# The first stage of a float32 transformer block: products on rows that are not scaled yet, and rows scaled ahead of the transposition

## The chip, the cores and the metric

One core of a Trainium2 chip runs the kernel. The metric is the device time of one execution, in microseconds (us); lower is better. Of the kernel before there are three timed runs, with a median of 1368.38 us (1367.94 to 1368.66), and one profiled execution.

## The reference

```python
h = rmsnorm(x, norm_w)              # x: (512, 2048) float32
proj = h @ w_in                     # w_in: (2048, IN_WIDTH), cut into eleven parts:
(a_q, a_f, a_i, a_g, c_q, c_kv, k_idx_raw, w_idx_raw, b_g, m_a, m_b) = split(proj)
y_a = hgrn2_branch(a_q, a_f, a_i, a_g, ...)   # gated linear recurrence, 8 heads
y_b = dsa_branch(c_q, c_kv, k_idx_raw, w_idx_raw, b_g, ...)   # indexed sparse attention
merged = sigmoid(m_a) * (y_a @ w_pa) + sigmoid(m_b) * (y_b @ w_pb)
return rmsnorm(x + merged @ w_out, final_norm_w)

def rmsnorm(x, w):
    return x * rsqrt(mean(x * x, axis=-1) + EPS) * w
```

All is float32. The first stage of the kernel computes `h`, transposed, and the first 272 columns it needs of `proj`: 256 of `a_i` (head pair 0) and the 16 of `w_idx_raw`.

## The kernel before, in words

**Numbers.** A float32 operand `a` is held as two parts that TensorE takes at one pass each: a high part (`high`, `w_high`: a rounding copy on ScalarE) and a low part, `a` minus the high part (`low`, `w_low`). A product is then three: high x high (here "hh"), low x high ("lh") and high x low ("hl"). In the stage, `xh` and `xl` hold the two parts of the normalised input, transposed, with 2048 channels in 16 blocks of 128 on the partitions; four blocks make a group `g`, 0 to 3. `wh` and `wl` hold those of the weights, again four blocks for each `i`.

**The first stage** is the function `start` (from L250 on). The 512 rows of `x` are four tiles `t` of 128 rows. Each tile is loaded in two halves (`xs[t][i]`, 512 KB each). A tile goes through these steps:

- `square`, `rstd` (L298 to L303): the sum of squares of its two halves on ScalarE, then a sum on VectorE and a root on ScalarE; `on_diag` takes the reciprocal and puts it on the diagonal of a 128x128 matrix.
- `turn` (L309 to L315): 16 transpositions on TensorE into four PSUM banks, one for each group.
- `spread` (L337 to L342): a product of a matrix of ones with the diagonal, so that the 128 row factors lie along the free dimension (`rrow`).
- the scaling on VectorE: each transposed element times its channel's weight `wc` (a column of `norm_w`) times its row's factor; the first tile does it in two steps (`weigh`, and `scaled` at L398), the others in one (L350, one instruction for each block, 16 for a tile).
- `high` on ScalarE and `low` (L324), for the tiles after the first on GpSimd for odd groups and on VectorE for even ones.
- `project` (L371 to L385): for each group, hh, lh and hl of four products each, 48 for a tile, into one PSUM bank; then the sums are moved out: 256 columns by ScalarE to `v` (L384) and 16 by VectorE to `widx` (L385).

`project(t)` writes the next tile's `follow(t + 1)` (its transpositions, spread, scaling, squares) between its second and its third group, so TensorE's queue holds 24 products of tile `t`, 16 transpositions and a spread of tile `t + 1`, and the other 24 products. In the last tile `prep(0)` stands there, which splits the weights of the next job.

**Order.** The program is compiled with a schedule by hand: every engine runs its instructions in the order in which the code writes them, and waits in that order where an operand is not ready. Semaphores come from the tiles' reads and writes.

**Loads.** All stand in SyncE's queue in this order: `norm_w`, tile 0 of `x`, weights 0 and 1, tile 1, weights 2 and 3, tiles 2 and 3, six small ones into `rows`, and the weights of the next job.

**Space.** TensorE's transpositions use a PSUM pool of four banks (`bank`), which also holds `warm`, a tile that four products of ones write ahead of the first load (L290 to L292). The sums use another four.

After the stage, `rows` is transposed (L432), and the jobs follow, which all read `xh` and `xl`.

Of the kernel before, what the change touches and what calls it, by code (L numbers as in the profile page):

```python
# [26 lines left out]
F32 = mybir.dt.float32  # L27
FR = mybir.dt.float32r
AF = mybir.ActivationFunctionType
OP = mybir.AluOpType  # L30
# [4 lines left out]
T, D = 512, 2048  # L35
# [15 lines left out]
def hybrid_block(ctx, tc, x, norm_w, w_in, lb_table, gnorm_a, q_norm_w, kv_norm_w, w_uq,  # L51
# [3 lines left out]
    V, A, G, PE, SP = nc.vector, nc.scalar, nc.gpsimd, nc.tensor, nc.sync  # L55
# [7 lines left out]
    mmp = ctx.enter_context(tc.tile_pool(name="mmp", bufs=4, space=PSUM))  # L63
# [4 lines left out]
    def bank(name):  # L68
        return sdp.tile([128, 512], F32, name=name, tag="sd")
# [10 lines left out]
    def mm(ps, l, r, first, last):  # L80
        PE.matmul(ps, l, r, start=first, stop=last, skip_group_check=True)  # L81
# [168 lines left out]
    def start():  # L250
        R.v0 = enter("v0")
        p0 = enter("p0", side="right")
        ident = p0.tile([128, 128], F32, name="ident")
        A.dma_start(ident, c_ident)
        HF = D // 2
        nw = p0.tile([16, 128], F32, name="nw")
        wc = p0.tile([128, 16], F32, name="wc")
        xs = [[p0.tile([128, HF], F32, name=f"x{t}{i}") for i in range(2)] for t in range(4)]
        ys = [p0.tile([128, 4, 128], F32, name=f"y{g}") for g in range(4)]
        diag = p0.tile([128, 128], F32, name="diag")  # L260
        sq = p0.tile([128, HF], mybir.dt.bfloat16, name="sq")
        st = p0.tile([128, 4, 4], F32, name="st")
        rows = p0.tile([128, 128], F32, name="rows")
        G.memset(rows, 1.0)
        G.tensor_copy(ones_r, rows)
        wh = [p0.tile([128, 4, 272], FR, name=f"fh{i}") for i in range(4)]
        wl = [p0.tile([128, 4, 272], FR, name=f"fl{i}") for i in range(4)]
        raw = [None] * 4

        def load_x(t):  # L270
            for i in range(2):
                SP.dma_start(xs[t][i], x2[t * 128:(t + 1) * 128, i * HF:(i + 1) * HF])

        def load_w(i):
            raw[i] = p0.tile([128, 4, 272], F32, name=f"fr{i}")
            for o, c0, c1 in ((0, 2048, 2304), (256, 4992, 5008)):
                SP.dma_start(raw[i][:, :, o:o + c1 - c0],
                             w_in[i * 512:(i + 1) * 512, c0:c1].rearrange("(k p) n -> p k n", p=128))

        SP.dma_start(nw, norm_w.rearrange("o (k d) -> (o k) d", d=128))  # L280
        load_x(0)
        load_w(0)
        load_w(1)
        load_x(1)
        load_w(2)
        load_w(3)
        load_x(2)
        load_x(3)
        A.activation(st[:, 0, 0:1], eps, AF.Sqrt)
        warm = bank("warm")  # L290
        for _ in range(4):
            PE.matmul(warm[:, 0:128], ones, ones, start=True, stop=True)  # L292
        G.memset(rows, 0.0)
        pw = mmp.tile([128, T], F32, name="acc")
        PE.transpose(pw[:, 0:16], nw, ident[0:16, 0:16])
        V.tensor_copy(wc, pw[:, 0:16])

        def square(t, i):  # L298
            A.activation(sq, xs[t][i], AF.Square, accum_out=st[:, t, i:i + 1])

        def rstd(t):
            V.tensor_add(st[:, t, 2:3], st[:, t, 0:1], st[:, t, 1:2])
            A.activation(st[:, t, 2:3], st[:, t, 2:3], AF.Sqrt, bias=eps, scale=1.0 / D)  # L303

        def on_diag(t):
            V.reciprocal(st[:, t, 3:4], st[:, t, 2:3])
            V.tensor_scalar(diag, ident, st[:, t, 3:4], None, op0=OP.mult)

        def turn(t, g):  # L309
            pt = bank("pt")  # L310
            for j in range(4):
                k = g * 4 + j
                PE.transpose(pt[:, j * 128:(j + 1) * 128],  # L313
                             xs[t][k // 8][:, (k % 8) * 128:(k % 8) * 128 + 128], ident)
            return pt  # L315

        def weigh(pt, g):
            V.tensor_tensor(ys[g], pt.rearrange("p (j t) -> p j t", j=4),
                            wc[:, g * 4:g * 4 + 4, None].to_broadcast([128, 4, 128]), op=OP.mult)

        def high(t, g):
            A.activation(xh[g][:, :, t * 128:t * 128 + 128], ys[g], AF.Copy)

        def low(t, g):  # L324
            o = slice(t * 128, t * 128 + 128)
            (G if t and g % 2 else V).tensor_tensor(xl[g][:, :, o], ys[g], xh[g][:, :, o].bitcast(F32),
                                                    op=OP.subtract)

        def w_high(i):
            A.activation(wh[i], raw[i], AF.Copy)  # L330

        def w_low(i, eng):
            eng.tensor_tensor(wl[i], raw[i], wh[i].bitcast(F32), op=OP.subtract)

        v = hg[0, "v"] = R.v0.tile([128, 4, 256], F32, name="hv")

        def spread():  # L337
            pr = mmp.tile([128, T], F32, name="acc")
            PE.matmul(pr[:, 0:128], ones, diag, start=True, stop=True)
            r = p0.tile([128, 128], F32, name="rrow", bufs=2)  # L340
            V.tensor_copy(r, pr[:, 0:128])
            return r  # L342

        def follow(t):
            pts = [turn(t, g) for g in range(4)]
            r = spread()

            def scaled(g):
                for j in range(4):
                    V.scalar_tensor_tensor(ys[g][:, j, :], pts[g][:, j * 128:j * 128 + 128],  # L350
                                           wc[:, g * 4 + j:g * 4 + j + 1], r, op0=OP.mult, op1=OP.mult)
                high(t, g)

            scaled(0)
            scaled(1)
            low(t, 0)
            if t < 3:
                square(t + 1, 0)
            scaled(2)
            low(t, 1)  # L360
            if t < 3:
                square(t + 1, 1)
            scaled(3)
            if t < 3:
                rstd(t + 1)
            low(t, 2)
            if t < 3:
                on_diag(t + 1)
            low(t, 3)

        def project(t):  # L371
            o = slice(t * 128, t * 128 + 128)
            acc = mmp.tile([128, T], F32, name="acc")
            for g in range(4):
                if g == 2:
                    if t < 3:
                        follow(t + 1)
                    else:
                        prep(0)
                for n, (xp, wp) in enumerate(((xh, wh), (xl, wh), (xh, wl))):  # L380
                    for k in range(4):
                        mm(acc[:, 0:272], xp[g][:, k, o], wp[g][:, k, :], g + n + k == 0,
                           g + n + k == 8)
            A.activation(v[:, t, :], acc[:, 0:256], AF.Copy)  # L384
            V.tensor_copy(widx[:, t, :], acc[:, 256:272])  # L385

        pts = [turn(0, g) for g in range(4)]
        weigh(pts[0], 0)
        weigh(pts[1], 1)
        square(0, 0)  # L390
        square(0, 1)
        rstd(0)
        on_diag(0)
        w_high(0)
        weigh(pts[2], 2)
        r = spread()

        def scaled(g):  # L398
            V.tensor_tensor(ys[g], ys[g], r[:, None, :].to_broadcast([128, 4, 128]), op=OP.mult)
            high(0, g)  # L400

        scaled(0)
        scaled(1)
        w_low(0, V)
        w_high(1)
        low(0, 0)
        weigh(pts[3], 3)
        square(1, 0)
        scaled(2)
        low(0, 1)  # L410
        scaled(3)
        w_low(1, V)
        w_high(2)
        w_low(2, V)
        square(1, 1)
        low(0, 2)
        rstd(1)
        low(0, 3)
        on_diag(1)
        w_high(3)  # L420
        w_low(3, G)
        SP.dma_start(rows[0:16], lb_table.rearrange("a (h d) -> (a h) d", d=128))
        SP.dma_start(rows[16:20], q_norm_w.rearrange("o (k d) -> (o k) d", d=128))
        SP.dma_start(rows[20:22], kv_norm_w.rearrange("o (k d) -> (o k) d", d=128))
        SP.dma_start(rows[22:23], kidx_norm_w)
        SP.dma_start(rows[23:24], kidx_norm_b)
        SP.dma_start(rows[24:25], gnorm_a)
        load_ahead()
        for t in range(4):
            project(t)  # L430
        pt = bank("pt")
        PE.transpose(pt[:, :128], rows, ident)  # L432
        V.tensor_copy(cols[:, 0:25], pt[:, :25])
        leave("p0")
# [1128 lines left out]
```

## Time and profile before

| | |
|---|---|
| median of three timed runs | 1368.38 us |
| profiled execution | 1367.72 us |
| its span, first to last instruction | 1365.8 us |
| TensorE, matmul busy | 1347.4 us |
| VectorE busy | 1075.2 us |
| ScalarE busy | 656.7 us |
| GpSimd busy | 81.2 us |
| transposition of `rows`, behind the first stage | starts at 46.67 us |

How to read the profile. It tells of one execution. Times count from the first instruction. PE is TensorE's matmul, PEld its weight loads, DVE is VectorE, ACT ScalarE, POOL GpSimd, SP the queue that issues the loads. A row of the timeline gives the start, the length, the engine, the line of the code (L313), the operation, what it writes and reads, how many neighbours of the kind are taken together (x16) and, in brackets, how long the engine sat idle before and what ended that. A group's row has the count, the busy time in us, the mean of one in ns, and the idle time before. The rows by stretches give, for each engine, busy us and instructions, then the granted clock of TensorE (1.00 is full), the share of DMA time and GB/s; where one engine is asked for, only that engine's figures stand. Ends of matmuls are modelled, so neighbouring ones overlap in the record.

### The profile page before, as it was taken

To read this page: it belongs to the slowest core of one execution; us is meant where nothing else is said; L and a number is where in the kernel's file an instruction comes from. 1 tells how busy PE (TensorE), PEld (TensorE's weight loads), DVE (VectorE), ACT (ScalarE), POOL (GpSimd) and SP (SyncE) were. 2 spreads that over 40 slices of the span, in tenths; PEclk is the share of its full clock that TensorE was granted. 3 is DMA by queue.
4 is the path that set the end of the run, shared out by engine and by line. 5 is a ranking of instruction groups with operands and counts; after the bars stand their busy time and mean duration, and the time that the engine had idled before them with its cause. 6 is when DMAs were issued, how large, how long until landed. Compare 5 with 4: busy or idle time off the path is not lost.

```text
span 1365.8 us, 26826 instructions
## 1 busy us (share of the span) xinstructions
PE 1347.4 (99%) x10940; PEld 1250.2 (92%) x10940; DVE 1075.2 (79%) x1741; ACT 656.7 (48%) x1054; POOL 81.2 (6%) x85
## 2 busy tenths in 40 slices
PE   8999999999999999999999999999999999999997
PEld 7888999999999999998999788888888888899996
DVE  7896889988898888876779989575556658899856
ACT  6555445545554444545745342645533334354444
POOL 2100000000000000000020303040101100000000
PEclk9999999999999999999999999999999999999999
DMA  6334345544444445446234423434856556643463
GB/s 207 93 109 138 103 146 168 157 139 140 139 144 123 122 138 155 140 139 196 72 103 140 134 72 121 125 116 144 303 162 201 197 173 220 211 144 121 163 239 139
DMA packets 145165, 204.79 MB, mean 150 GB/s; under 512 B 10585, under 2 KB 87058, under 8 KB 144914
## 3 DMA queue, kind: packets, MB, share of 16 engines
q1 hardware_dynamic: 144754, 202.82, 47.2%
q8 instruction: 86, 1.41, 0.4%
q14 instruction: 37, 0.30, 0.1%
q10 hardware_dynamic: 288, 0.26, 0.1%
HBM read 167.89 MB, written 35.15 MB: 149 GB/s over the span
## 4 chain that ended last, share of the span: by engine, by line
PE 94%; DVE 3%; ACT 2%; DMA 1%; issue 1%; SPq 0%; ACTq 0%; DVEq 0%
PE pp L77 15%; PE pp L78 15%; PE pp L76 15%; PE acc L76 13%; PE acc L78 13%; PE acc L77 13%; PE acc L81 1%; PE hl L81 1%; PE ho L81 1%; DVE wl L73 1%; DMA wr<-in_w_qidx_dram 1%; PE sc L76 1%; PE sc L77 0%; PE sc L78 0%; PE pt L313 0%
## 5 line engine op out<-in xcount | busy, mean ns | idle before, releaser
L150 ACT ACTIVATE bh<-wr 128x768 fp32r<-128x768 f32 x128 | 108.2, 845 | 218.3 <-issue 105.4
L152 ACT ACTIVATE wh<-sv 128x512 fp32r<-128x512 f32 x256 | 151.8, 623 | 85.3 <-DVE sv L145 66.0
L73 DVE TENSOR_TENSOR wl<-wr,wh 128x1024 fp32r<-128x1024 f32 (+1 forms) x104 | 127.6, 1228 | 59.9 <-ACT wh L72 59.5
L76 PE MATMUL pp<-s,wh 128*128 128x256 f32 x624 | 172.3, 276 | 0.0
L77 PE MATMUL pp<-s,wh 128*128 128x256 f32 x624 | 172.3, 276 | 0.0
L78 PE MATMUL pp<-s,wl 128*128 128x256 f32 x624 | 172.3, 276 | 0.0
L154 DVE TENSOR_TENSOR wl<-sv,wh 128x1024 fp32r<-128x1024 f32 x128 | 156.4, 1222 | 7.3 <-ACT wh L152 1.1
L153 DVE TENSOR_TENSOR bl<-wr,bh 128x768 fp32r<-128x768 f32 x128 | 122.2, 955 | 50.4 <-ACT bh L150 50.4
L72 ACT ACTIVATE wh<-wr 128x1024 fp32r<-128x1024 f32 (+1 forms) x104 | 108.0, 1040 | 106.5 <-PE acc L77 60.2
L76 PE MATMUL acc<-xh,wh 128*128 128x512 f32 x304 | 121.7, 400 | 0.0
L78 PE MATMUL acc<-xh,wl 128*128 128x512 f32 x304 | 118.7, 391 | 0.0
L77 PE MATMUL acc<-xl,wh 128*128 128x512 f32 x304 | 118.5, 390 | 0.0
L77 PEld LDWEIGHTS pp<-s,wh 128*128 128x128 f32 x624 | 117.2, 188 | 0.0
L76 PEld LDWEIGHTS pp<-s,wh 128*128 128x128 f32 x624 | 117.1, 188 | 0.0
L78 PEld LDWEIGHTS pp<-s,wl 128*128 128x128 f32 x624 | 117.1, 188 | 0.0
L76 PE MATMUL pp<-xh,bh 128*128 128x256 f32 x416 | 114.9, 276 | 0.0
L78 PE MATMUL pp<-xh,bl 128*128 128x256 f32 x416 | 114.9, 276 | 0.0
L77 PE MATMUL pp<-xl,bh 128*128 128x256 f32 x416 | 114.9, 276 | 0.0
L76 PE MATMUL acc<-yh,wh 128*128 128x512 f32 x256 | 100.2, 391 | 0.0
L78 PE MATMUL acc<-yh,wl 128*128 128x512 f32 x256 | 99.8, 390 | 0.0
L77 PE MATMUL acc<-yl,wh 128*128 128x512 f32 x256 | 99.7, 390 | 0.0
L145 DVE TENSOR_TENSOR sv<-wr 128x512 f32<-128x512 f32 x128 | 87.8, 686 | 10.6 <-DMA wr<-in_w_in_dram 7.1
(391 smaller groups left out, 3687.9 us busy)
## 6 DMA issues: line engine op xcount, KB each, us to landing
wr<-in_w_in_dram SPq DMA_DIRECT2D x136, 512.0 KB, 3.7
wr<-in_w_out_dram SPq DMA_DIRECT2D x32, 512.0 KB, 3.7
mg<-gate_d SPq DMA_DIRECT2D x48, 256.0 KB, 4.9
gate_d<-c SPq DMA_DIRECT2D x44, 256.0 KB, 5.1
wr<-in_w_in_dram SPq DMA_DIRECT2D x36, 256.0 KB, 2.7
wr<-in_w_pa_dram SPq DMA_DIRECT2D x16, 512.0 KB, 5.8
wr<-in_w_pb_dram SPq DMA_DIRECT2D x16, 512.0 KB, 4.4
x<-in_x_dram SPq DMA_DIRECT2D x8, 512.0 KB, 4.4
```

What stands on the lines that cost most here:

```text
L72: A.activation(hi, src, AF.Copy)
L73: V.tensor_tensor(lo, src, hi.bitcast(F32), op=OP.subtract)
L76: PE.matmul(ps, lh, rh, start=first, stop=False, skip_group_check=True)
L77: PE.matmul(ps, lh, rl, start=False, stop=False, skip_group_check=True)
L78: PE.matmul(ps, ll, rh, start=False, stop=last, skip_group_check=True)
L81: PE.matmul(ps, l, r, start=first, stop=last, skip_group_check=True)
L145: V.tensor_tensor(sv[:, 0:2, :], b[:, 1:3, :], b[:, 0:1, :].to_broadcast([128, 2, 256]), op=OP.add)
L150: A.activation(bh, b[:, 1:4, :], AF.Copy)
L152: A.activation(vh[:, i:i + 2, :], sv[:, i:i + 2, :], AF.Copy)
L153: V.tensor_tensor(bl, b[:, 1:4, :], bh.bitcast(F32), op=OP.subtract)
L154: V.tensor_tensor(vl, sv, vh.bitcast(F32), op=OP.subtract)
```

## The change

- **Tile 0**: its transposed rows are weighted by `norm_w` only, split, and multiplied; the row factor is applied to the sums when they are moved out (`scale=` on ScalarE, a multiplication on VectorE). Since later jobs need `xh` and `xl` of the scaled rows, tile 0 is scaled and split a second time (`spread`, `scaled`, `low`) while tiles 2 and 3 are worked on.
- **Tiles 1 to 3**: `row` multiplies 512 channels of the loaded rows by the row's factor and by `nb`, `norm_w` spread over all partitions by a load of its own; `turn` transposes the result, and `high` and `low` read PSUM.
- All lows are on VectorE, also the one of weight 3.
- `keep_busy(4)` issues four more products of ones at three places.
- The products' order is written out with `use` and `pairs`; products of tile 0 with low weights are partly put behind those of tile 1.
- `prep(0)` stands ahead of the products of tile 3.

```diff
+        nb = p0.tile([128, D], F32, name="nb")
...
         load_w(2)
+        SP.dma_start(nb, norm_w.to_broadcast([128, D]))
         load_w(3)
...
+        def keep_busy(n):
+            for _ in range(n):
+                PE.matmul(warm[:, 0:128], ones, ones, start=True, stop=True)
+
+        keep_busy(4)
...
+        def inverse(t):
             V.reciprocal(st[:, t, 3:4], st[:, t, 2:3])
-            V.tensor_scalar(diag, ident, st[:, t, 3:4], None, op0=OP.mult)
...
+        def row(t, g):
+            n = slice(g % 2 * 512, g % 2 * 512 + 512)
+            V.scalar_tensor_tensor(xs[t][g // 2][:, n], xs[t][g // 2][:, n], st[:, t, 3:4], nb[:, g * 512:g * 512 + 512],
+                                   op0=OP.mult, op1=OP.mult)
 
         def high(t, g):
-            A.activation(xh[g][:, :, t * 128:t * 128 + 128], ys[g], AF.Copy)
+            A.activation(xh[g][:, :, t * 128:t * 128 + 128], wide(t, g) if t else ys[g], AF.Copy)
 
         def low(t, g):
             o = slice(t * 128, t * 128 + 128)
-            (G if t and g % 2 else V).tensor_tensor(xl[g][:, :, o], ys[g], xh[g][:, :, o].bitcast(F32),
-                                                    op=OP.subtract)
+            V.tensor_tensor(xl[g][:, :, o], wide(t, g) if t else ys[g], xh[g][:, :, o].bitcast(F32), op=OP.subtract)
...
+        def use(t, *parts):
+            if t not in accs:
+                accs[t], done[t] = mmp.tile([128, T], F32, name="acc"), 0
+            o = slice(t * 128, t * 128 + 128)
+            for kind, g in parts:
+                xp, wp = {"hh": (xh, wh), "lh": (xl, wh), "hl": (xh, wl)}[kind]
+                for k in range(4):
+                    mm(accs[t][:, 0:272], xp[g][:, k, o], wp[g][:, k, :], done[t] == 0 and k == 0, done[t] == 11)
+                done[t] += 1
+            if done[t] == 12:
+                if t:
+                    A.activation(v[:, t, :], accs[t][:, 0:256], AF.Copy)
+                    V.tensor_copy(widx[:, t, :], accs[t][:, 256:272])
+                else:
+                    A.activation(v[:, t, :], accs[t][:, 0:256], AF.Copy, scale=st[:, 0, 3:4])
+                    V.tensor_scalar(widx[:, t, :], accs[t][:, 256:272], st[:, 0, 3:4], None, op0=OP.mult)
+
+        def pairs(t, gs):
+            use(t, *((kind, g) for g in gs for kind in ("hh", "lh", "hl")))
+
         def spread():
+            V.tensor_scalar(diag, ident, st[:, 0, 3:4], None, op0=OP.mult)
             pr = mmp.tile([128, T], F32, name="acc")
             PE.matmul(pr[:, 0:128], ones, diag, start=True, stop=True)
-            r = p0.tile([128, 128], F32, name="rrow", bufs=2)
             V.tensor_copy(r, pr[:, 0:128])
...
+        turn(0)
+        keep_busy(4)
+        weigh(0)
+        high(0, 0)
+        weigh(1)
+        high(0, 1)
+        low(0, 0)
+        weigh(2)
+        w_high(0)
+        high(0, 2)
+        low(0, 1)
+        weigh(3)
+        high(0, 3)
         w_high(1)
-        low(0, 0)
-        weigh(pts[3], 3)
+        low(0, 2)
+        low(0, 3)
         square(1, 0)
+        square(1, 1)
+        w_low(0)
+        w_low(1)
+        rstd(1)
+        inverse(1)
         w_high(2)
         w_high(3)
-        w_low(3, G)
+        use(0, ("hh", 0), ("lh", 0), ("hh", 1), ("lh", 1))
+        keep_busy(4)
+        use(0, ("hl", 0), ("hl", 1), ("hh", 2), ("lh", 2))
+        for g in range(4):
+            row(1, g)
+        turn(1)
+        use(0, ("hh", 3), ("lh", 3))
+        high(1, 0)
+        high(1, 1)
+        low(1, 0)
+        w_low(2)
+        high(1, 2)
+        low(1, 1)
+        square(2, 0)
+        high(1, 3)
+        low(1, 2)
+        low(1, 3)
+        square(2, 1)
+        w_low(3)
+        rstd(2)
+        inverse(2)
+        square(0, 0)
+        square(0, 1)
+        for g in range(4):
+            row(2, g)
+        rstd(0)
+        inverse(0)
...
         load_ahead()
-        for t in range(4):
-            project(t)
+        pairs(1, (0, 1))
+        use(1, ("hh", 2), ("lh", 2))
+        use(0, ("hl", 2))
+        use(1, ("hl", 2), ("hh", 3), ("lh", 3))
+        turn(2)
+        use(0, ("hl", 3))
+        use(1, ("hl", 3))
+        for g in range(4):
+            high(2, g)
+            low(2, g)
+            if g % 2:
+                square(3, g // 2)
+        spread()
+        rstd(3)
+        inverse(3)
+        scaled(0)
+        scaled(1)
+        low(0, 0)
+        low(0, 1)
+        for g in range(4):
+            row(3, g)
+        pairs(2, (0, 1, 2))
+        turn(3)
+        scaled(2)
+        for g in range(4):
+            high(3, g)
+            low(3, g)
+        scaled(3)
+        low(0, 2)
+        low(0, 3)
+        pairs(2, (3,))
+        prep(0)
+        pairs(3, range(4))
         pt = bank("pt")
         PE.transpose(pt[:, :128], rows, ident)
```

More of the change, by code (lines that the diff above doesn't have):

```diff
@@ L303, in rstd @@
             A.activation(st[:, t, 2:3], st[:, t, 2:3], AF.Sqrt, bias=eps, scale=1.0 / D)
-        def on_diag(t):
+        def inverse(t):
             V.reciprocal(st[:, t, 3:4], st[:, t, 2:3])
[L307 to L315, printed above, removed]
@@ L317, in weigh, with turn @@
-        def weigh(pt, g):
-            V.tensor_tensor(ys[g], pt.rearrange("p (j t) -> p j t", j=4),
-                            wc[:, g * 4:g * 4 + 4, None].to_broadcast([128, 4, 128]), op=OP.mult)
+        pts, accs, done = {}, {}, {}
+        def turn(t):
+            for g in range(4):
+                pts[t, g] = bank("pt")
+                for j in range(4):
+                    k = g * 4 + j
+                    PE.transpose(pts[t, g][:, j * 128:(j + 1) * 128],
+                                 xs[t][k // 8][:, (k % 8) * 128:(k % 8) * 128 + 128], ident)
@@ L321, in high, with wide, weigh @@
+        def wide(t, g):
+            return pts[t, g].rearrange("p (j t) -> p j t", j=4)
+        def weigh(g):
+            V.tensor_tensor(ys[g], wide(0, g), wc[:, g * 4:g * 4 + 4, None].to_broadcast([128, 4, 128]), op=OP.mult)
+        def row(t, g):
+            n = slice(g % 2 * 512, g % 2 * 512 + 512)
+            V.scalar_tensor_tensor(xs[t][g // 2][:, n], xs[t][g // 2][:, n], st[:, t, 3:4], nb[:, g * 512:g * 512 + 512],
+                                   op0=OP.mult, op1=OP.mult)
         def high(t, g):
-            A.activation(xh[g][:, :, t * 128:t * 128 + 128], ys[g], AF.Copy)
+            A.activation(xh[g][:, :, t * 128:t * 128 + 128], wide(t, g) if t else ys[g], AF.Copy)
@@ L324, in low, with w_low @@
         def low(t, g):
             o = slice(t * 128, t * 128 + 128)
-            (G if t and g % 2 else V).tensor_tensor(xl[g][:, :, o], ys[g], xh[g][:, :, o].bitcast(F32),
-                                                    op=OP.subtract)
+            V.tensor_tensor(xl[g][:, :, o], wide(t, g) if t else ys[g], xh[g][:, :, o].bitcast(F32), op=OP.subtract)
         def w_high(i):
             A.activation(wh[i], raw[i], AF.Copy)
-        def w_low(i, eng):
-            eng.tensor_tensor(wl[i], raw[i], wh[i].bitcast(F32), op=OP.subtract)
+        def w_low(i):
+            V.tensor_tensor(wl[i], raw[i], wh[i].bitcast(F32), op=OP.subtract)
@@ L337, in spread @@
+        def pairs(t, gs):
+            use(t, *((kind, g) for g in gs for kind in ("hh", "lh", "hl")))
         def spread():
+            V.tensor_scalar(diag, ident, st[:, 0, 3:4], None, op0=OP.mult)
             pr = mmp.tile([128, T], F32, name="acc")
             PE.matmul(pr[:, 0:128], ones, diag, start=True, stop=True)
-            r = p0.tile([128, 128], F32, name="rrow", bufs=2)
             V.tensor_copy(r, pr[:, 0:128])
[L342 to L396, printed above, removed]
+        r = p0.tile([128, 128], F32, name="rrow")
         def scaled(g):
@@ L400, in scaled @@
             high(0, g)
-        scaled(0)
-        scaled(1)
-        w_low(0, V)
+        turn(0)
[11 more added lines that the diff above has]
+        high(0, 3)
         w_high(1)
-        low(0, 0)
-        weigh(pts[3], 3)
+        low(0, 2)
+        low(0, 3)
         square(1, 0)
[L409 to L412, printed above, removed]
-        w_high(2)
[L414 to L419, printed above, removed]
-        w_high(3)
-        w_low(3, G)
+        square(1, 1)
[3 more added lines that the diff above has]
+        inverse(1)
+        w_high(2)
+        w_high(3)
+        use(0, ("hh", 0), ("lh", 0), ("hh", 1), ("lh", 1))
[25 more added lines that the diff above has]
+        inverse(0)
         SP.dma_start(rows[0:16], lb_table.rearrange("a (h d) -> (a h) d", d=128))
@@ L428, in start @@
         load_ahead()
-        for t in range(4):
-            project(t)
+        pairs(1, (0, 1))
[22 more added lines that the diff above has]
+        scaled(2)
+        for g in range(4):
+            high(3, g)
[6 more added lines that the diff above has]
+        pairs(3, range(4))
         pt = bank("pt")
```

## The prediction

> **What bounds the kernel now**
>
> I read four views: the page's head with the chain that ended last, then busy time by stretches, TensorE's line of the timeline in the first 47 us, and the groups of instructions of the first 50 us.
>
> ```profile
> span 1365.8 us, 26826 instructions
> ...
> PE 1347.4 (99%) x10940; PEld 1250.2 (92%) x10940; DVE 1075.2 (79%) x1741; ACT 656.7 (48%) x1054; POOL 81.2 (6%) x85
> ...
> PE 94%; DVE 3%; ACT 2%; DMA 1%; issue 1%; SPq 0%; ACTq 0%; DVEq 0%
> ```
> ```profile
> 5.00:10.00 5.00, 4.15 (x18) 3.57 (x18) 2.64 (x7) 3.63 (x6) 0.00 (x0) 1.00 1.11 353
> ...
> 20.00:46.70 26.70, 26.43 (x213) 25.86 (x212) 22.17 (x69) 14.32 (x28) 10.37 (x7) 1.00 0.10 27
> 46.70:1365.80 1319.10, 1307.09 (x10669) 1211.57 (x10666) 1040.71 (x1650) 630.05 (x1007) 69.88 (x70) 1.00 0.48 150
> ```
>
> TensorE (PE) is busy 99% of the span and carries 94% of the last chain. The diff touches the first stage alone, which ends at 46.67 us, where the transposition of `rows` starts (fence below). Behind it PE is busy for 1307.09 of 1319.10 us, and that work stays the same. So what counts is when PE reaches that point. The profiled execution took 1367.72 us, its span 1365.8; the median of the three runs, 1368.38, is 0.66 above it. I make the sum against 1367.72 and add 0.66 at the end.
>
> ```profile
> 5.64 3.67 PE L313 MATMUL pt<-ident,x 128*128 128x128 f32 x16 [1.97 <-DMA x<-in_x_dram]
> 9.31 0.49 PE L339 MATMUL acc<-diag,ones_r 128*128 128x128 f32 x2
> 11.57 0.77 PE L81 MATMUL acc<-fh,xh 128*128 128x272 f32 x4 [1.77 <-ACT xh L322]
> 13.31 1.27 PE L81 MATMUL acc<-fh,xl 128*128 128x272 f32 x4 [0.97 <-DVE xl L326]
> ...
> 15.29 1.11 PE L81 MATMUL acc<-fh,xh 128*128 128x272 f32 x4
> 16.20 1.11 PE L81 MATMUL acc<-fh,xl 128*128 128x272 f32 x4
> ...
> 18.01 2.64 PE L313 MATMUL pt<-ident,x 128*128 128x128 f32 x16
> ...
> 20.63 0.74 PE L81 MATMUL acc<-fh,xh 128*128 128x272 f32 x4
> ...
> 26.93 1.91 PE L313 MATMUL pt<-ident,x 128*128 128x128 f32 x16
> ...
> 46.67 0.27 PE L432 MATMUL pt<-ident,rows 128*128 128x128 f32 x1
> ```
> ```profile
> 1.18 4.42 DMA x<-in_x_dram
> ...
> 37.77 9.06 PE acc L81 x72
> ```
> ```profile
> 12.00:13.00 1.00, 0.34 (x3) 0.84 1.09 373
> 13.00:14.00 1.00, 0.69 (x3) 0.50 1.20 301
> ...
> 19.00:20.00 1.00, 1.00 (x9) 0.75 1.03 410
> ```
>
> PE's unit prices come from these rows. At full clock a product (L81) costs 9.06 / 72 = 0.126 us; at half clock the next four start 0.91 later (15.29, 16.20), so 0.227. A transposition at full clock is 0.109: sixteen take 1.91, of which the last record is about 0.27 long, so 1.64 / 15. The row at 5.64 has 3.67 for the same sixteen, 0.21 each. The view by stretches gives full clock from 5 to 10 us (1.00), but these durations say half; the granted clock is evidently not recorded so early. After 3.7 us of transposing, the four products of 11.57 are fast (0.77). Then PE idles, the clock falls at about 12.7 (0.84 of 12 to 13 us, 0.50 after) and comes back at 19.5, though PE worked on from 13.31: 6.2 us after it resumed. The stage before thus loses its time up to 20 us, to the wait for scaled halves and to the clock. From 20.6 to 46.67 PE is nearly dense (26.43 of 26.70 us), so little is left to win there.
>
> **The change part by part**
>
> ScalarE (ACT) and VectorE (DVE) prices:
>
> ```profile
> L322 ACT ACTIVATE xh<-y 128x512 fp32r<-128x512 f32 x16 | 10.1, 631 | 12.6 <-DVE y L350 10.6 <-DVE y L399 2.0
> ...
> L299 ACT ACTIVATE sq<-x 128x1024 bf16<-128x1024 f32 x8 | 8.4, 1045 | 3.1 <-DMA x<-in_x_dram 3.0
> L326 POOL TENSOR_TENSOR xl<-y,xh 128x512 fp32r<-128x512 f32 x6 | 7.8, 1305 | 13.9 <-ACT xh L322 13.9
> L326 DVE TENSOR_TENSOR xl<-y,xh 128x512 fp32r<-128x512 f32 x10 | 6.8, 682 | 0.0
> L330 ACT ACTIVATE fh<-fr 128x1088 fp32r<-128x1088 f32 x4 | 4.4, 1097 | 0.0
> L333 DVE TENSOR_TENSOR fl<-fr,fh 128x1088 fp32r<-128x1088 f32 x3 | 3.9, 1284 | 0.5 <-ACT fh L330 0.5
> L318 DVE TENSOR_TENSOR y<-pt,wc 128x512 f32<-128x512 f32 x4 | 2.7, 687 | 3.1 <-PE pt L313 3.1
> ...
> L333 POOL TENSOR_TENSOR fl<-fr,fh 128x1088 fp32r<-128x1088 f32 x1 | 2.5, 2537 | 19.1 <-ACT fh L330 19.1
> ...
> L384 ACT ACTIVATE hv<-acc 128x256 f32<-128x256 f32 x4 | 1.5, 364 | 0.0
> ```
> ```profile
> L573 DVE SCALAR_TENSOR_TENSOR c<-c,cols,rq 128x512 f32<-128x512 f32 x4 | 3.0, 746 | 0.0
> ```
> ```profile
> 6.80 0.69 DVE L318 TENSOR_TENSOR y<-pt,wc 128x512 f32<-128x512 f32 x1 [2.91 <-PE pt L313]
> ...
> 8.97 0.28 DVE L307 TENSOR_SCALAR diag<-ident,st 128x128 f32<-128x128 f32 x1
> ```
> ```profile
> 25.61 1.04 ACT L299 ACTIVATE sq<-x 128x1024 bf16<-128x1024 f32 x1
> ...
> 26.64 0.62 ACT L322 ACTIVATE xh<-y 128x512 fp32r<-128x512 f32 x1
> 26.77 0.16 DVE L302 TENSOR_TENSOR st<-st 128x1 f32<-128x1 f32 x1 [0.70 <-ACT sq L299]
> ...
> 27.17 0.28 ACT L303 ACTIVATE st<-st,cols 128x1 f32<-128x1 f32 x1
> ...
> 27.35 0.36 ACT L384 ACTIVATE hv<-acc 128x256 f32<-128x256 f32 x1
> 27.48 0.16 DVE L306 RECIPROCAL st<-st 128x1 f32<-128x1 f32 x1
> ```
>
> A high half costs 0.63 (L322), a low half 0.68 (L326 on DVE), a weight's high half 1.10 and low half 1.28, an eviction 0.36. A square with its read-out costs 1.03 (25.61 to 26.64). Sum, root and reciprocal take 0.87 from 26.77 to the end of L306 at 27.64. The new `row` instruction is not in this trace; its nearest row has the same form, 128x512 in SBUF times a column times a tensor: L573, 0.746. The bounds are 0.68 (L318, two operands) and 0.75; I take 0.746. Each engine runs in the order of the code: at 26.64 to 27.35 ACT does `high(1,3)`, the root for tile 2 and then tile 0's eviction, exactly as `follow` and `project` write them.
>
> *Removed:* for tiles 1 to 3 the scaling behind the transposition, the three spreads and their diagonals; the lows on GpSimd (six of 1.3 us, beside other work) and the weight low of 2.54 there move to DVE: 6 x 0.68 + 1.28 = 5.4 us more. *Added:* twelve rows (8.95 us), `nb` (1 MB, on SP's queue ahead of `w3` and the loads of tiles 2 and 3), twelve extra warming products in three groups, and tile 0's highs and lows a second time. The first two warming groups lie where PE waits for data, the third lies before weight low 0; I cost them at nothing, 0.9 us each if that cover went. The warming tile now lives until the third group and holds a PSUM bank, so the fourth transposed group has to wait for `weigh(0)`, which ends about when PE gets there: nothing to 0.5 us, and I take nothing.
>
> *To 21.9 us.* `weigh(0)` starts at 6.8 as before, then ACT does two highs and weight high 0, to 10.1: PE's first product comes at 10.2 instead of 11.57. But it has only four groups of four products before weight high 1 (ACT: high 2, high 3, then 1.10, to 12.9) and weight high 2, which queues behind two squares and a root (to 16.9).
>
> ```profile
> GB/s 0 85 223 331 356 352 362 343 406 374 328 337 364 413 403 413 119 201 182 56 0 0 0 0 0 0 0 7 0 0 13 0 0 0 0 0 0 109 304 6
> ```
>
> The loads set the rest. Each figure of this row is 1.25 us. Up to the end of `w2` stand two tiles of `x` (1.05 MB each), three weights (0.56 each) and 0.07 MB of small ones, 3.84 MB, which the row has moved by 13.4 us. The first half tile of `x` landed at 5.60 (1.18 + 4.42), 1.2 us after the row had moved its 0.60 MB, so `w2` lands at 14.6. `nb` then needs 1.05 MB / 0.38 = 2.8 us, to 17.4, and `w3` 1.5 more, to 18.9. (If reading one 8 KB row 128 times is slower than `x` was, up to 1.5 times, `nb` adds 1.4; I know no reason for a gain.) DVE's four rows of tile 1 end at 17.4 + 2.98 = 20.4, PE's last four transpositions at 20.9, and with weight high 3 (18.9 + 1.1 = 20.0) the next two groups at 21.9. By then PE has done 40 products and 32 transpositions; before, it had 24 at 20.6, so about 34 at 21.9. The whole lead is some 0.8 us.
>
> *To 31.3 us.* ACT's `high(1,0)` stands behind weight high 3, to 20.6. DVE goes on at 20.7: a low, weight low 2, three lows, weight low 3 (4 x 0.68 + 2 x 1.28 = 5.3, to 26.0), sum to reciprocal (26.9), rows of tile 2 (2.98, to 29.9). PE's 48 products from 21.9 end at 27.9; it waits for the rows, finishes `turn(2)` at 30.3, and two more groups (1.0) at 31.3.
>
> *The new wait.* The spread for tile 0 now stands in PE's queue ahead of all products of tile 2. Its diagonal is on DVE behind the four lows of tile 2, these follow the four highs on ACT, and those stand behind the evictions of tiles 0 and 1, which need the very products that end at 31.3. So from there: about 0.2 until the last sum can be read (a product's record is 0.16 longer than its spacing), eviction 0.36, highs 4 x 0.63 with one square 1.03 between, 3.9 in all, to 35.4; the last low 0.68, the diagonal 0.28, to 36.4. PE idles 5.1 us, and nothing else of its queue can run. This chain starts from PE itself, so no faster load shortens it. Behind PE's spread are queued 96 products and 16 transpositions.
>
> *The rest.* 0.2 + 96 x 0.126 + 16 x 0.109 = 14.0 us; at full clock PE would reach the end at 50.4. But an idle stretch of 5 us is longer than the pauses that cost the clock at 12.7. Back to full speed took 6.2 us after 13.31, and at least 3.5 after 5.64 (slow until 9.1). Each half-clocked us loses 1 - 0.126/0.227 = 0.445, so 1.6 to 2.8; I take the middle, 2.2, with nothing and 2.8 as ends: 52.6. What could be late next is not: DVE does spread copy, root, two scalings, two lows and the rows of tile 3 by 43.8, when PE is at about 43.6; from there the lows of tile 3, two scalings and the last lows of tile 0 take it to about 50.7, and `prep(0)`'s first weight follows with one low more, before 52.6.
>
> The Trainium skill's "TensorE: Matmul & The Clock Gate", Part 1, says that the clock is set by free-running windows of 3.4 us, full after a busy one, half after an idle one. The trace agrees: 12.7 to 19.5 is 6.8, two such windows. By that alone the slow stretch after the wait would be 3.4 to 6.8 us, about the same sum.
>
> *Sum.* 52.6 - 46.67 = +5.9 us: 1367.72 + 5.9 = 1373.6 for the profiled execution, **1374.3** as a median.
>
> **The rivals**
>
> *The clock is lost in more places.* Between 11 and 21 us PE waits three times (weight highs 1 and 2, `nb`) and is busy for little over half of it. For: before, the fall at 12.7 came with 0.49 + 0.77 busy since 9.3. Against: that is 37%, here it is 55 to 60%, and the warming products fill one wait. If the clock falls there as well, 8 products to a us become 4.4 up to 23 or 26 us; DVE's chain hides 2 us of it, and 1 to 3 remain, and the recovery after 36.4 may need a second attempt (1.5). Median 1375.5 to 1379.
>
> Part 4 of the same page of the Trainium skill says that transpositions don't count as busy for this gate, which speaks for this rival, since `turn(1)` is most of what PE does between 18 and 21. The trace speaks against it: 3.67 us of transpositions alone were followed by fast products.
>
> *The wait is covered.* If ACT and DVE did tile 2's halves while PE is still at tile 1, PE would go from 31.3 without a break: 31.3 + 14.0 = 45.3, 1.4 less than now, 1367.0, no measurable change. Against: the order of the queues, which the rows at 26.64 to 27.35 show.
>
> *Faster.* With that wait covered and no delay from `nb` and `w3` (rows of tile 1 right after their reciprocal, at 12.9 + 2 x 1.03 + 0.87 = 15.8 rather than 17.4, and weight high 3 as soon as ACT gets to it) the lead grows by 2 us more: 43.3, a median of 1365.0. It decides from the point where the diagonal is ready before PE's last product of tile 1, 5.1 us earlier than I find. That the dense stretch from 20 to 46.7 was already PE's own work speaks against more.
>
> **How the numbers follow**
>
> Forecast 0.68, clock lost in more places 0.20, wait covered 0.07, faster 0.05. A measurement of this kernel tells 0.2%, 2.7 us, from no change. The first two are slower: 0.88. The range goes from 1371.8 (no slow clock after the wait: 50.4, so 1372.1, and the small steps 0.3 shorter) to 1379, the end of the second case.
>
> **What would show it**
>
> In the changed kernel: first product at about 10.2; `nb` awaited by DVE near 17.4; tile 1's last product near 31; then an idle PE of about 5 us released by the diagonal (DVE, the line of `spread`); a granted clock of 0.5 for 3 to 6 us from about 33 to 40; the stage's end at 52 to 53. I am wrong if tile 2's products start within a us of tile 1's end, or if PE gets to that place much later than 32 us.

## The result, and the profile after

The changed kernel takes 1376.3 us as the median of six runs (1374.95 to 1378.06), the kernel before 1368.14 beside it: a ratio of 1.0061 (95% interval 1.0050 to 1.0071). It is slower, by 8.2 us; the forecast was 1374.3, in a range of 1371.8 to 1379.0. The profiled execution of after took 1375.92 us, its span 1374.1, which is 8.3 more than before. I take the span apart where the transposition of `rows` starts, the end of the stage: before, 46.67 and then 1319.13 us; after, 51.38 and then 1322.72. So 4.7 us come from the stage, and 3.6 from code that the diff doesn't touch.

First the view by stretches of after, for all engines (PE, PEld, DVE, ACT, POOL: busy us and instructions; then granted clock, DMA share, GB/s), and the same view of before for the stretch behind the stage.

```profile
10.00:20.00 10.00, 8.20 (x48) 7.42 (x48) 6.94 (x12) 6.51 (x11) 0.00 (x0) 0.83 1.06 380
20.00:51.38 31.38, 26.81 (x204) 26.27 (x203) 23.90 (x44) 18.40 (x37) 0.00 (x0) 0.95 0.19 60
51.38:1374.10 1322.72, 1308.88 (x10669) 1213.83 (x10667) 1040.03 (x1650) 630.76 (x1007) 69.27 (x70) 1.00 0.48 149
```
```profile
46.67:1365.80 1319.13, 1307.12 (x10669) 1211.60 (x10667) 1040.71 (x1650) 630.05 (x1007) 69.88 (x70) 1.00 0.48 150
```

From 20 us on, PE was busy for all but 0.3 us of the stage before; now 4.6 us of 31.38 are idle, and the mean clock is 0.95. Behind the stage PE has the same 10669 instructions, but it is busy 1.8 us longer and idle 1.8 us longer (13.84 against 12.01).

The timeline of after, the rows that answer to the steps of the prediction:

```profile
10.43 0.78 PE L81 MATMUL acc<-fh,xh 128*128 128x272 f32 x4 [0.96 <-ACT fh L345]
...
17.88 2.74 DVE L334 SCALAR_TENSOR_TENSOR x<-x,st,nb 128x512 f32<-128x512 f32 x4 [2.47 <-DMA nb<-in_norm_w_dram]
...
19.55 1.11 ACT L345 ACTIVATE fh<-fr 128x1088 fp32r<-128x1088 f32 x1 [3.20 <-DMA fr<-in_w_in_dram]
...
29.97 1.25 PE L81 MATMUL acc<-fl,xh 128*128 128x272 f32 x8
...
31.54 1.08 ACT L338 ACTIVATE xh<-pt 128x512 fp32r<-128x512 f32 x2
...
35.38 0.28 DVE L373 TENSOR_SCALAR diag<-ident,st 128x128 f32<-128x128 f32 x1
...
35.71 0.49 PE L375 MATMUL acc<-diag,ones_r 128*128 128x128 f32 x2 [4.49 <-DVE diag L373]
...
36.54 1.10 PE L81 MATMUL acc<-fh,xl 128*128 128x272 f32 x4
...
51.38 0.27 PE L476 MATMUL pt<-ident,rows 128*128 128x128 f32 x1
```

`nb` is awaited by VectorE to 17.88; tile 1's last products run to 31; then PE stands still for 4.49 us until the diagonal of tile 0 is there. From 36.54 on, four products take 1.10 us instead of 0.66: the clock has fallen. PE's line of the view by stretches shows that, and a second fall far behind the stage:

```profile
30.50:36.50 6.00, 1.51 (x12) 1.00 0.01 3
36.50:40.00 3.50, 3.50 (x18) 0.51 0.00 0
40.00:51.40 11.40, 11.40 (x95) 1.00 0.07 16
...
647.50:651.00 3.50, 3.50 (x14) 0.51 0.26 92
```

The list of PE's waits, of before and then of after (total us, times, longest), shows that waits behind the stage have grown too: the one for `sc`, a PSUM tile of a later job, from 1.6 to 2.8 us at its longest, and one for `bf`, a load of a later job, that was not there.

```profile
PE sc L76 <- ACT relu L653: 2.2, 2, 1.6
PE pt L313 <- DMA x<-in_x_dram: 2.0, 1, 2.0
```
```profile
PE acc L375 <- DVE diag L373: 4.5, 1, 4.5
PE sc L76 <- ACT relu L697: 3.2, 2, 2.8
...
PE t L81 <- DMA bf<-t_d: 0.7, 1, 0.7
```

### The profile page after: what moved, and what is told of

Read it like the earlier page. It is cut to its first block, busy times and chain, and to the rows that moved or that the text cites. A ratio compares the mean times of both kernels' runs of the same rounds, so it can differ in the third digit from the quotient of the medians.

```text
span 1374.1 us, 26835 instructions
## 1 busy us (share of the span) xinstructions
PE 1351.3 (98%) x10958; PEld 1253.9 (91%) x10958; DVE 1074.0 (78%) x1710; ACT 659.1 (48%) x1058; POOL 70.2 (5%) x78
## 3 DMA queue, kind: packets, MB, share of 16 engines
q8 instruction: 86, 1.41, 0.4%
HBM read 168.94 MB, written 35.15 MB: 149 GB/s over the span
## 4 chain that ended last, share of the span: by engine, by line
PE 93%; DVE 2%; ACT 2%; DMA 2%; issue 1%; SPq 0%; ACTq 0%; DVEq 0%
PE pp L77 15%; PE pp L76 15%; PE pp L78 15%; PE acc L76 13%; PE acc L78 13%; PE acc L77 13%; PE acc L81 2%; PE hl L81 1%; PE ho L81 1%; DVE wl L73 1%; DMA wr<-in_w_qidx_dram 1%; PE sc L76 1%; PE sc L77 0%; PE sc L78 0%; DMA fr<-in_w_in_dram 0%
```

## The experiments

All start from the changed kernel unless it is said otherwise. "PE instructions ahead" are all that the traces show of PE before the transposition of `rows`: the products and their weight loads, and 12 or 19 others, nearly all for semaphores. Ratios are to the kernel before, run beside each, with 95% intervals. Stage end and rest are those of one profiled execution; the runs of one kernel spread over 1.1 to 4.0 us, so a row by itself tells little below a us.

| kernel | PE instructions ahead | stage end | rest of the span | profiled | median of the runs | ratio |
|---|---|---|---|---|---|---|
| before | 559 | 46.67 | 1319.1 | 1367.72 | 1368.14 | |
| after | 602 | 51.38 | 1322.7 | 1375.92 | 1376.3 | 1.0061 (1.0050 to 1.0071) |
| spread_first | 602 | 49.72 | 1322.8 | 1374.28 | 1373.96 | 1.0047 (1.0035 to 1.0060) |
| warm_wait | 666 | 49.95 | 1321.8 | 1373.56 | 1373.96 | 1.0046 (1.0032 to 1.0060) |
| few_warm | 558 | 51.74 | 1318.7 | 1372.28 | 1371.6 | 1.0028 (1.0017 to 1.0040) |
| before_padded | 601 | 49.38 | 1323.0 | 1374.37 | 1374.37 | 1.0050 (1.0037 to 1.0062) |
| few_warm_padded | 602 | 50.10 | 1322.3 | 1374.16 | 1374.55 | 1.0052 (1.0038 to 1.0066) |
| one_block_more | 814 | 59.40 | 1318.7 | 1379.86 | (one run, no interval) | |
| reordered | 558 | 44.52 | 1318.9 | 1365.26 | 1365.6 | 0.9982 (0.9974 to 0.9991) |

**1. The wait: spread_first.** The diagonal and its product come ahead of the last products of tiles 0 and 1.

```
         turn(2)
+        spread()
         use(0, ("hl", 3))
         use(1, ("hl", 3))
...
-        spread()
         rstd(3)
```

> The changed kernel with spread() written ahead of tile 0's and tile 1's last groups instead of behind tile 2's halves. Stage (start of the transposition of rows: 46.67 before, 51.38 after): if the wait for the diagonal carries it, the pause of 4.5 us shrinks to the eviction and one high, 1.2 to 1.5, the clock stays at full speed, and the stage ends at 46 to 47.5. If VectorE is the bound anyway, it ends above 49. Rest (from there to the end of the span: 1319.1 before, 1322.7 after): PE's instructions keep their count, so if the rest lost 3.6 us because PE's code blocks are fetched at other places, it stays at 1321 to 1324; if it lost them because all came 4.7 us later, it returns to 1319 to 1320. Median 1369.5 to 1372.5 by the first, 1367.5 to 1369 by the second.

Measured: stage end 49.72, 1.66 us earlier. The timeline says where the rest of the 4.5 went (VectorE's rows in the second fence).

```profile
29.66 0.49 PE L375 MATMUL acc<-diag,ones_r 128*128 128x128 f32 x2 [0.20 <-DVE diag L373]
...
32.11 0.77 PE L81 MATMUL acc<-fh,xh 128*128 128x272 f32 x4 [0.96 <-ACT xh L338]
...
39.66 2.66 PE L323 MATMUL pt<-ident,x 128*128 128x128 f32 x16 [2.55 <-issue]
```
```profile
17.13 2.74 DVE L334 SCALAR_TENSOR_TENSOR x<-x,st,nb 128x512 f32<-128x512 f32 x4 [1.93 <-DMA nb<-in_norm_w_dram]
...
36.23 1.27 DVE L381 TENSOR_TENSOR y<-y,rrow 128x512 f32<-128x512 f32 x2
37.60 1.29 DVE L342 TENSOR_TENSOR xl<-y,xh 128x512 fp32r<-128x512 f32 x2
38.81 2.73 DVE L334 SCALAR_TENSOR_TENSOR x<-x,st,nb 128x512 f32<-128x512 f32 x4
```

PE comes to tile 2's products at 32.11 instead of 35.95, and is then held for 2.55 us in front of the transpositions of tile 3. The profile names no releaser ("issue"), but the first of them runs 0.85 us after VectorE starts the rows of tile 3, which stand behind two scalings and two lows of tile 0. The wait for the diagonal is real, but with it gone VectorE's order sets the pace: the wait moves rather than ends. This is the second of the two outcomes expected (above 49). The clock shows no fall here; the longest idle stretch behind 20 us is 2.55. Not all of the 1.66 us is the edit's: `nb` lands earlier in this execution, so that the rows of tile 1, which stand ahead of the edit, start at 17.13 and not at 17.88.

**2. The clock: warm_wait.** Sixteen products of ones stand in the wait, ahead of the diagonal's product. They change nothing in the order; they keep PE busy.

```
             pr = mmp.tile([128, T], F32, name="acc")
+            for _ in range(16):
+                PE.matmul(pr[:, 128:256], ones, ones, start=True, stop=True)
             PE.matmul(pr[:, 0:128], ones, diag, start=True, stop=True)
```

> The changed kernel with 16 products of ones in PE's queue just ahead of the spread's product, so that PE works through most of the wait for the diagonal. The wait stays (the product of the diagonal starts at 35.5 to 36). If the half clock of 36.5 to 40 costs 1.5 us, the stage ends at 49.6 to 50.2; if VectorE's rows of tile 3 would have come late anyway, at 51 or more. PE has 64 instructions more, so the rest can be anything between 1319 and 1323 by the code blocks, 1322 to 1323 by the later start.

```profile
30.50 3.73 PE L376 MATMUL acc<-ones_r 128*128 128x128 f32 x32
35.15 0.49 PE L377 MATMUL acc<-diag,ones_r 128*128 128x128 f32 x2 [0.92 <-DVE diag L373]
39.98 2.59 PE L323 MATMUL pt<-ident,x 128*128 128x128 f32 x16
```
The last row's counterpart in after:

```profile
42.08 1.91 PE L323 MATMUL pt<-ident,x 128*128 128x128 f32 x16
```

The diagonal's product comes at 35.15 (35.71 in after), the record of the clock shows full speed from 6.3 us to the end of PE's work, and the stage ends at 49.95, 1.4 us earlier. Of that, 0.56 is the earlier product, and no effect of the edit: here too `nb` lands earlier, and the rows of tile 1 start at 17.31 (17.88 in after). The slow window of after, 3.4 us, is worth 3.4 x 0.445 = 1.5 by the prediction's prices; 0.7 of it is given back where the transpositions of tile 3 take 2.59 instead of 1.91 us, as PE now comes to them sooner than VectorE has the rows (experiment 1 shows the same wait). So 0.56 + 1.5 - 0.7 = 1.4: the fall of the clock cost about what one window costs, and VectorE stands right behind.

**3. The missing 3.6 us: few_warm.** Of the twelve added products of ones, one is left. That takes 44 instructions from PE's program, and moves no other step.

```
-        keep_busy(4)
+        keep_busy(1)
...
         turn(0)
-        keep_busy(4)
...
         use(0, ("hh", 0), ("lh", 0), ("hh", 1), ("lh", 1))
-        keep_busy(4)
```

> The changed kernel with one warming product instead of twelve. PE then executes 44 instructions fewer ahead of the rest, and the rest starts at the same place of a code block as before the change, within an instruction or two. If the place of the code blocks is what the rest lost 3.6 us by, the rest returns to 1319 to 1320.5; if the later start, another layout of memory or the late prep(0) did it, it stays near 1322.7. Stage: the warming products are either worth something through the clock (stage end 52 to 54 without them) or nothing (51.4).

```profile
51.74:1370.40 1318.66, 1306.64 (x10669) 1211.66 (x10667) 1041.44 (x1650) 629.72 (x1007) 70.03 (x70) 1.00 0.48 150
```

The stage is 0.36 us longer: the clock is low from 33.54 to 40.37, twice as long as in after, and five us of that lie behind the wait. Yet the profiled time is 3.6 us shorter: behind the stage the time is back at 1318.66 (0.3 below what was expected), and PE's idle time there at 12.0 us. What the changed kernel loses behind its stage thus has nothing to do with its new order of steps.

**4. The other way round: before_padded.** The kernel *before*, with 21 small products of ones ahead of the first transposition, 42 PE instructions.

```
         V.tensor_copy(wc, pw[:, 0:16])
+        for _ in range(21):
+            mm(warm[:, 0:16], ones_r, ones_r[:, 0:16], True, True)
```

> The kernel before with 21 products of 16 columns (42 instructions of PE) in PE's idle time ahead of the first load, whose result nobody reads. Stage end 46 to 47.3. If the place of PE's code blocks sets the loss in the rest, the rest goes from 1319.1 to 1321 to 1324 and the median to 1370 to 1372.5, though nothing else is changed; by the other theories the rest stays within 0.5 of 1319.1 and the median within 1 of the kernel before.

```profile
49.38:1372.40 1323.02, 1307.78 (x10669) 1211.62 (x10667) 1040.46 (x1650) 630.00 (x1007) 68.94 (x70) 1.00 0.48 149
```

The stage loses 2.7 us, since the small products run to 8.1 us and so delay the transpositions by 2.5; an end at 46 to 47.3 was expected, and for that the median lies above its 1370 to 1372.5. But the rest, whose code and order are those of before, loses 3.9 more. So the loss can be made without any part of the change.

**5. The count put back: few_warm_padded.** few_warm, and eleven products of ones (44 instructions) in the wait for the diagonal, as in warm_wait.

```
+            for _ in range(11):
+                PE.matmul(pr[:, 128:256], ones, ones, start=True, stop=True)
             PE.matmul(pr[:, 0:128], ones, diag, start=True, stop=True)
```

> The version with few warming products, and 11 full-size products of ones more, issued in the stretch in which PE waits for the diagonal anyway; PE then executes 602 instructions ahead of the transposition of the norms' rows again, as in the changed kernel (few_warm 558, before 559). Theory (what the rest of the program lost hangs on how many PE instructions precede it, since PE's code comes in blocks of 256 instructions and a fetch beside a burst of loads holds up the load): the rest goes back from 1318.7 to about 1322.5 us, and the stage, whose clock the added products hold up, ends at 50 to 51.7; profiled time 1374.5 to 1376. Rival (the rest was lost to the warming products themselves or to when the stage ends): the rest stays at 1318.7 and the time is 1370.5 to 1372.3, not above few_warm's 1372.28.

```profile
50.10:1372.38 1322.28, 1307.43 (x10669) 1211.76 (x10667) 1038.69 (x1650) 630.28 (x1007) 69.86 (x70) 1.00 0.48 150
```
```profile
PE sc L76 <- ACT relu L697: 2.8, 2, 2.6
...
PE ns L81 <- DVE suml L73: 1.0, 1, 1.0
PE t L81 <- DMA bf<-t_d: 0.9, 1, 0.9
```

The stage ends 1.6 us earlier than in few_warm, and the kernel is slower by 1.9 in its profiled execution: the rest goes back to 1322.28, and the waits for `sc` and `bf` are back, much as in after (in few_warm 1.6 at the longest for `sc`, and none for `bf`). The profiled time, 1374.16, is 0.3 below what was expected. The rival, that the warming products themselves or the moment of the stage's end cost the time, is out.

**6. One whole block: one_block_more.** PE's code is read in by the DMA queue q8, 16 KB at a time: 86 packets, 1.41 MB, for some 22,000 PE instructions, so about 256 instructions a packet. In all nine traces packet n, counted from 0, starts when PE has begun 256 n instructions and some 150 to 430 more. If what counts is where the borders of these blocks fall in the later program, 256 more instructions must do nothing. So: few_warm with `range(64)` in place of `range(11)`.

> The version with few warming products and 64 full-size products of ones before the diagonal's product, 256 PE instructions: one whole block of code more than few_warm (814 ahead of the transposition of the norms' rows, 558 there). The products take about 64 x 0.24 = 15 us, 4.5 of which lie in the wait, so the stage ends near 60 to 62 us; only the rest of the span is looked at. Theory A (what counts is where the borders of the blocks of 256 fall in the later program): the borders are where few_warm has them, the rest is 1318.7 again, within 0.7. Theory B (any added instructions, or any products issued into the wait, cost the rest some 3.5 us): 1321.8 to 1323.1. Theory C (a later stage end shifts the rest against loads that run by their own): a rest that differs from both, above all below 1318.

The queue's line of the page of few_warm, the same line of this kernel, and then its view by stretches:

```profile
q8 instruction: 86, 1.41, 0.4%
```

```profile
q8 instruction: 87, 1.43, 0.4%
```
```profile
59.40:1378.08 1318.68, 1306.90 (x10669) 1211.75 (x10667) 1040.17 (x1650) 630.03 (x1007) 70.21 (x70) 1.00 0.48 150
```

One packet more (87), a stage that is 7.7 us longer (its end, 59.40, is 0.6 short of the 60 to 62 expected), and a rest of 1318.68, level with few_warm's 1318.66. Forty-four instructions cost the rest 3.6 us, 256 cost it nothing. For 256 there is only this one execution, but it agrees to 0.02 us, with a stage that ends later than in any other version; so the rest's loss does not follow the moment at which the stage ends.

**7. A version that uses it: reordered.** few_warm with another order: tile 0's squares first of all (ScalarE is idle up to the first high), the diagonal and its product between tile 0's first products, three scalings in VectorE's wait for `nb`, the highs and lows of tile 2 ahead of the last products that end in evictions, rows of tile 3 ahead of tile 0's second lows. The squares of tile 3 and weight high 3 move as well. The edit, in part:

```
+        square(0, 0)
+        square(0, 1)
         turn(0)
...
+        V.tensor_scalar(diag, ident, st[:, 0, 3:4], None, op0=OP.mult)
         square(1, 0)
...
         w_high(2)
-        w_high(3)
         use(0, ("hh", 0), ("lh", 0), ("hh", 1), ("lh", 1))
+        spread()
         use(0, ("hl", 0), ("hl", 1), ("hh", 2), ("lh", 2))
+        for g in range(3):
+            scaled(g)
         for g in range(4):
             row(1, g)
+        w_high(3)
...
         turn(2)
-        use(0, ("hl", 3))
-        use(1, ("hl", 3))
         for g in range(4):
             high(2, g)
             low(2, g)
-            if g % 2:
-                square(3, g // 2)
-        spread()
-        rstd(3)
+        use(0, ("hl", 3))
+        use(1, ("hl", 3))
         inverse(3)
-        scaled(0)
-        scaled(1)
-        low(0, 0)
-        low(0, 1)
         for g in range(4):
             row(3, g)
+        scaled(3)
+        for g in range(4):
+            high(0, g)
```

(Here `spread` makes only the product and its copy, and `scaled` only the scaling; the second highs of tile 0 follow the rows of tile 3.)

> The changed kernel with one product of warming instead of twelve and another order on VectorE and ScalarE: squares of tile 0 first, the diagonal and its product between tile 0's first products, three of the scalings while VectorE waits for the norm's rows, highs and lows of tile 2 ahead of the evictions, rows of tile 3 ahead of tile 0's second lows. Theory (the stage's gain in the change was eaten by one wait for the diagonal and by an order that makes VectorE the bound later): no PE wait over 1 us after 16 us, stage end 44.5 to 47 us (after 51.38, before 46.67); with 558 PE instructions ahead of the rows' transposition the rest is 1318.7 to 1319.1; profiled time 1365.2 to 1368.0, level with before or up to 0.2% under it. Rival A (the new order's work on VectorE does not fit in whatever order, 2.7 us of lows made twice and 2.7 us of rows per tile): stage end 48.5 to 50, time 1369 to 1371. Rival B (the rest loses in any version that scales tile 0 afterwards): rest 1322.7, time 1369.5 to 1371.5 with a stage of 45 to 47.

```profile
20.00:44.52 24.52, 24.44 (x200) 24.23 (x199) 20.44 (x37) 15.04 (x32) 0.00 (x0) 1.00 0.29 91
44.52:1363.38 1318.86, 1306.83 (x10669) 1212.08 (x10667) 1041.06 (x1650) 630.35 (x1007) 70.73 (x70) 1.00 0.48 150
```
```profile
14.30 0.39 PE L374 MATMUL acc<-diag,ones_r 128*128 128x128 f32 x2
...
29.60 1.25 PE L81 MATMUL acc<-fl,xh 128*128 128x272 f32 x8
30.69 0.67 PE L81 MATMUL acc<-fh,xh 128*128 128x272 f32 x4
...
35.22 1.91 PE L323 MATMUL pt<-ident,x 128*128 128x128 f32 x16
```

From 20 us on PE is idle for 0.08 us, the diagonal's product stands at 14.30 with nothing waiting for it, tile 2's products (30.69) follow tile 1's without a break, and the clock is full: the theory's outcome on every count. The stage ends at 44.52, 2.2 us before that of the kernel before, and the rest is 1318.86. The median is 1365.6 over eleven runs, a ratio of 0.9982: faster than both kernels, though by only 2.5 us (0.2%) than the kernel before. Scaling the rows ahead of the transposition was not what made the change slower.

## Why the prediction came out as it did

*To 21.9 us*: right in its steps. The first product came at 10.43 (10.2), `nb` at 17.88 (17.4), weight 3 at 19.55 (18.9). With `nb` in SP's queue VectorE waited for 2.47 us and ScalarE for 3.20.

*To 31.3 us*: right; the last products of tile 1 end at 31.2.

*The new wait*: right in its chain, 4.5 us instead of 5.1. Two highs from PSUM take 1.08 us together (they start 0.48 apart), not 2 x 0.63 as the row of before had it, and only one square stood among them, as counted.

*The rest, clock*: one slow window, 36.53 to 39.95, 3.42 us, is 1.5 by the prediction's prices; 2.2 had been taken as the middle of 1.6 to 2.8. Full speed was back 4.2 us after PE resumed (35.71 to 39.95), within the 3.5 to 6.2 taken, and the first 0.8 of these ran at full clock. In few_warm the same wait of 4.49 us was followed by 5.0 us at half clock (35.40 to 40.37), worth 2.2 by the same prices; so the length of the wait does not fix the figure. The Trainium skill's "TensorE: Matmul & The Clock Gate", Part 1, has free-running windows of 3.4 us, and the records agree: 3.4 us in after at 36.5 and at 647.5, and 6.8 before.

*Sum*: the stage, +5.9 by the prediction, was +4.7 (some 0.6 of the difference is the wait, 0.7 the clock).

*The step that failed* is the one in front of all: "Behind it PE is busy for 1307.09 of 1319.10 us, and that work stays the same. So what counts is when PE reaches that point." The work stayed, its time did not: +3.6 us, from 43 instructions more ahead of it. The twelve warming products, which the prediction costed at nothing, are 48 instructions (12 went with three spreads, and 7 more came, for semaphores); with eleven of them out, the loss is gone (experiment 3). Together 4.7 + 3.6 = 8.3 stands against 5.9. The forecast's median was only 2.0 too low, and that is partly luck: the stage was overestimated and the rest taken as unchanged. With the stage's true +4.7 the same sum gives 1373.1, 3.2 too low.

*"What could be late next is not"* (the rows of tile 3 done by 43.8, when PE gets there): it held for the changed kernel, whose rows of tile 3 end at 42.3, while PE begins their transpositions at 42.08, one row after the other. But it had no room, as spread_first shows: with PE earlier, VectorE was late by 2.55 us.

*The rivals.* The clock was lost at one more place ahead of the wait (12.64 to 16.05; PE was busy for 1.64 of the 3.42 us ahead of that, 48%, where the prediction had reckoned with 55 to 60%), but less than before, and the rival's price did not come: PE had to wait for the rows of tile 1 behind it anyway (0.48 us idle ahead of 18.73). "The wait is covered" and "faster" asked for the diagonal 5.1 us earlier; the order did not give it. In reordered the first of them comes true: tile 2's products start at 30.69 and the stage ends 13.8 us later (the rival had 31.3 + 14.0 = 45.3). The other also asked for rows of tile 1 at 15.8; there `nb` keeps them to 17.57, so its 43.3 was not tried.

**What stays open.** How the block borders cost time is seen only as a coincidence in the records. In after, a packet of q8 runs at 637.37, while two loads of `w_qidx` are under way (issued at 633.8 and 634.3, awaited until 643.42); in few_warm at 643.09, behind them. ScalarE's row for these weights:

```profile
643.42 1.06 ACT L72 ACTIVATE wh<-wr 128x1024 fp32r<-128x1024 f32 x1 [2.75 <-DMA wr<-in_w_qidx_dram]
```
```profile
642.69 1.06 ACT L72 ACTIVATE wh<-wr 128x1024 fp32r<-128x1024 f32 x1 [1.61 <-DMA wr<-in_w_qidx_dram]
```

The first is of after, the second of few_warm, where the same load is awaited for 1.1 us less. In after the clock falls right behind this wait (647.5 to 651). Of the 3.6 us that its rest lost against before, 1.8 are busy time of PE, about what a slow window costs, and 1.8 idle time; in few_warm_padded, where the record shows no such fall, it is 0.8 and 2.8 against few_warm. So the loss is not made up alike in each execution.

Before and few_warm_padded fit the coincidence: in before the packet comes at 638.58, behind the landing, and ScalarE idles for 1.61 us; in few_warm_padded it comes at 637.41, and the idle time is 2.56. But in spread_first a packet runs at 636.14, also while these loads are under way, and the load is awaited for only 1.53 us. In spread_first, before_padded and warm_wait PE waits for `relu` 0.7 to 0.9 us longer just ahead of it, and the sum is lost all the same, in steps of about 0.3 to 1 us, most of them near 65, 640, 720 and 825. That a fetch holds up a load is thus a guess. Shown is that the rest follows the number of instructions ahead: with 558, 559 and 814, which leave 46 or 47 when divided by 256, it is 1318.7 to 1319.1; with 601, 602 and 666, which leave 89, 90 and 154, it is 2.7 to 4.3 us longer.

## What to carry to other kernels

Before a stage's gain or loss is read from the total, split the span at the stage's end: here two causes of about the same size stood in one number, and only one of them lay in the code that the diff touches. When code is added to or taken from the front of a long program, compare the untouched part by itself, and if it moved, pad the engine's instructions to the old place before the change is judged. And when a wait is taken away, look at what the next engine in the chain does in that time: spread_first won 1.7 us of the stage at most, where the wait had been 4.5; with the order on VectorE and ScalarE changed as well (reordered), the stage won 6.9. Last, look at the instructions ahead of an edit too: where they start at other times than in the run compared with, as `nb` let them here by up to 0.75 us, that part is not the edit's.

## What the runs showed of the hardware

- PE's code comes in packets of 256 instructions (86 for some 22,000, 87 with 256 more), all along the execution (in after from 24 to 1361 us). Where the later program stands against these blocks was worth 2.7 to 4.3 us of 1319: 1318.7 to 1319.1 with 558, 559 and 814 instructions ahead, 1321.8 to 1323.0 with 601, 602 and 666. The Trainium skill's "Trainium Architecture — The Big Picture", The software stack, gives an instruction 64 bytes, which fits 256 to a packet of 16 KB.
- Idle stretches of 4.5 us went with a low clock for 3.4 us (after) or for 6.8 (few_warm, 33.54 to 40.37); in spread_first, 2.55 us of idle time took none. The length of a pause is not all that counts: after and spread_first have the same instructions up to 28 us, and only in after did the clock fall at 12.64, with no pause longer than 0.96 us just ahead of it (1.13 in spread_first).
- In warm_wait 3.73 us of useless products ahead of a wait of 0.92 us went with a full clock throughout, at no cost to the path.
- Four `scalar_tensor_tensor` of 128x512 in SBUF take 2.74 us in a row, 0.69 each, though one alone is recorded with 0.75, as the row that the estimate used: they start 0.66 apart.
